# A sliding-window copy with twelve staged batches, half-row direct copies and the remainders on SP's queue

## The chip, the core and the metric

The kernel runs on one core of a Trainium2 chip. It does no arithmetic: it only moves data with DMAs, which 16 DMA engines of the core carry out. Three sequencers issue the DMAs: SP (SyncE) and ACT (ScalarE) each feed a hardware queue, POOL (GpSimd) feeds a queue whose descriptors are written by software. All three queues run on the same 16 engines. The metric is the device time of one execution in microseconds; less is better.

## The reference

The input x has 32 batches of 4096 rows of 256 float32 values (134 MB). Windows of 64 rows start every 32 rows, 127 of them per batch, and each is copied out.

```python
n_windows = (length - window_size) // stride + 1      # 127
for i in range(n_windows):
    start = i * stride                                # stride 32
    result[:, i] = x[:, start:start + window_size]    # window 64
```

The output is 32 x 127 x 64 x 256 float32, 266.3 MB. A batch is 128 blocks of 32 rows (32 KB each). Window w is block w followed by block w + 1, so each block but the first and last is written twice: as the first half of one window and as the second half of the one before it.

## The kernel before

**Two ways to copy a batch.** A *direct* batch is copied from HBM to HBM. A row of such a DMA is one window, 64 KB in one piece on both sides (Copier.windows with half=None), and the engines move it as two packets of 32 KB (DIRECT). Windows can also be copied by halves: one DMA for the first halves of a group of windows and one for the second halves (half 0 and 1), with rows of 32 KB, one packet each. A direct batch reads each block twice. A *staged* batch is loaded to SBUF once, in a tile of 128 partitions, one block to each (Copier.load, rows of 32 KB in packets of 16 KB, IN), and stored twice, once as all first halves and once as all second halves (Copier.store, packets of 16 KB, OUT).

**Which batches.** Eleven batches are staged: 1, 4, 7, ..., 28 and 30. The other 21 are direct. Staged batches go on ACT's queue, direct ones on SP's.

**The spill.** A staged store writes all 128 blocks as first halves and all 128 as second halves, though there are only 127 windows. The last first half falls on window 0 of the next batch, and the first second half on window 126 of the batch before. Those windows hold wrong bytes until the direct neighbour writes them, so the neighbour must write them after the staged store has landed. A direct batch therefore has 7 chunks of 16 windows that touch no spill (112 windows), and a *remainder* of 15 windows at the end or at the beginning (rest_parts), which waits for the staged neighbour's stores (waits, Staging.wait_stored). The last staged batch doesn't spill: it is stored in pieces of 112, 15, 15 and 112 rows. In the kernel before this is batch 30.

**Staging on ACT's queue.** There are 6 tiles. Staging.run goes through the staged batches in groups of 6: all loads of a group, then all its stores. A load into a used tile waits until that tile's stores have landed; a store waits for its load.

**Direct copies on SP's queue.** SP issues the 7 chunks of each of the 21 direct batches in order and doesn't wait. A running count, share, decides whether a chunk goes as one DMA of whole windows (1024 KB) or two DMAs of halves (512 KB each): by halves in 9 of 12 while the count of turns falls in the stretch of loads, in 3 of 12 otherwise. A *turn* here is one packet that an engine takes from the queue; the small packet that marks a DMA as complete is one too. So a chunk as a whole takes 2 + 1 turns on each engine, by halves 2 x (1 + 1).

**Remainders on POOL's queue.** When the chunk third from the end has landed (semaphore near), POOL issues the 21 remainders, 15 windows (960 KB) each, in the order of the staged batches that they wait for. SP ends with waits for everything: the direct copies (done), POOL's remainders (soft) and the last staged batch (last).

Of the kernel before, what the change touches and what calls it, by code (L numbers as in the profile page):

```python
# [6 lines left out]


DIRECT, IN, OUT = 32768, 16384, 16384
PIECES = (32768,)  # L10


class Copier:


    def __init__(self, nc, tc, x, out, B, L, D, W, S, n_win):
        assert W == 2 * S and L % S == 0
        self.nc, self.tc, self.x, self.out = nc, tc, x, out
        self.B = B
        self.blk = S * D  # L20
        self.nb = L // S
        self.nw = n_win
        self.total = 0
        self.done = tc.alloc_semaphore("done")
        self.last = tc.alloc_semaphore("last")
        self.last_total = 0

    def xap(self, block, dims):
        return bass.AP(self.x.tensor, self.x.offset + block * self.blk, dims)
# [4 lines left out]
    def count(self, dma):  # L34
        dma.then_inc(self.done, 16)
        self.total += 16

    def count_last(self, dma):
        dma.then_inc(self.last, 16)
        self.last_total += 16  # L40

    def windows(self, q, b, w0, n, half=None, piece=DIRECT, count=None):

# [21 lines left out]
    def store(self, q, t, b, half, p0=0, n=None):  # L65

        blk = self.blk
        n = self.nb if n is None else n  # L70
        w = b * self.nw + p0 - half
        return q.dma_start(
            out=self.oap(w * 2 * blk + half * blk, [[2 * blk, n], [1, blk]]),
            in_=t[p0 : p0 + n, :],
            max_dma_last_dim=OUT,
        )


class Staging:
# [14 lines left out]
    def store(self, q, g):  # L94
        n, i = divmod(g, len(self.tiles))
        q.wait_ge(self.loaded[i], 16 * (n + 1))
        if g == len(self.batches) - 1:

            for half, p0, rows in ((0, 0, 112), (0, 112, 15), (1, 1, 15), (1, 16, 112)):
                self.c.count_last(self.c.store(q, self.tiles[i], self.batches[g], half, p0, rows))  # L100
            return
        for half in (0, 1):
            self.c.store(q, self.tiles[i], self.batches[g], half).then_inc(self.stored[i], 16)
# [15 lines left out]
@with_exitstack  # L119
def kernel(  # L120
    ctx: ExitStack,
    tc: tile.TileContext,
    x: bass.AP,
    window_size: bass.AP,
    stride: bass.AP,
    out: bass.AP,
):
    nc = tc.nc
    W, S = int(window_size), int(stride)
    B, L, D = x.shape  # L130
    n_win = (L - W) // S + 1
    assert out.shape == (B, n_win, W, D)
    c = Copier(nc, tc, x, out, B, L, D, W, S, n_win)
    staged = [*range(1, B - 3, 3), B - 2]
    direct = [b for b in range(B) if b not in staged]
    pool = ctx.enter_context(tc.tile_pool(name="xb", bufs=1))
    st = Staging(c, pool, x.dtype, staged, 6)
    ring_d, ring_s = nc.sync, nc.scalar
    spilled = staged[:-1]

    waits = {b: [g for g, n in enumerate(spilled) if abs(n - b) == 1] for b in direct}
    per, loads, stores = 6, 6 * 17, 34

    def first(b):
        return 0 if b - 1 not in spilled else 8 if len(waits[b]) == 2 else 15

    def rest_parts(b):
        if len(waits[b]) == 2:
            return [(0, 8), (120, 7)]
        return [(0 if b - 1 in spilled else 112, 15)]  # L150

    soft = tc.alloc_semaphore("soft")
    soft_total = 0

    near = tc.alloc_semaphore("near")

    def mark(dma):
        dma.then_inc(near, 16)

    def count_soft(dma):  # L160
        nonlocal soft_total
        dma.then_inc(soft, 16)
        soft_total += 16

    with tc.tile_critical():  # L165
        st.run(ring_s)

        turns = share = 0
        rests = []
        todo = 7 * len(direct)  # L170
        for b in direct:
            for j in range(7):
                at = turns % (loads + per * stores)
                share += 9 if at < loads else 3
                if share >= 12:
                    share -= 12
                    turns += 4
                    c.windows(ring_d, b, first(b) + 16 * j, 16, 0)
                    c.windows(ring_d, b, first(b) + 16 * j, 16, 1, count=mark if todo == 3 else None)
                else:  # L180
                    turns += 3
                    c.windows(ring_d, b, first(b) + 16 * j, 16, count=mark if todo == 3 else None)
                todo -= 1
            rests.append(b)

        ring_r = nc.gpsimd
        ring_r.wait_ge(near, 16)
        for i, b in enumerate(sorted(rests, key=lambda b: max(waits[b], default=0))):
            for g in waits[b]:
                st.wait_stored(ring_r, g)  # L190
            for w, n in rest_parts(b):
                c.windows(ring_r, b, w, n, None, PIECES[i % 1], count_soft)
        ring_d.wait_ge(c.done, c.total)
        ring_d.wait_ge(soft, soft_total)
        ring_d.wait_ge(c.last, c.last_total)


# [33 lines left out]
```

## Time and profile before

| | |
|---|---|
| time, three runs | 745.32, 745.44, 745.96 us (median 745.44) |
| the profiled execution | 745.32 us |
| its span | 743.5 us |
| bytes moved by the DMA engines | 313.16 MB in 18,092 packets |
| HBM read / written | 220.92 / 266.99 MB |
| SP's DMAs | 83 of 1024 KB, 128 of 512 KB |
| ACT's DMAs | 11 loads and 20 stores of 4096 KB, 2 stores of 3584 KB, 2 of 480 KB |
| POOL's DMAs | 21 of 960 KB |

The page cuts the span in 40 slices and gives for each the busy share of the 16 DMA engines in tenths, and the GB/s that they moved. A byte that goes from HBM to HBM counts once in those bytes, but is one byte read and one written for HBM. The queue table gives for each queue its packets, its bytes and the time that its packets took, as a share of 16 engines times the span. q1 is SP's queue, q10 is ACT's and q0 is POOL's. Packets under 512 bytes are the completion marks. The same tables can be asked of any stretch of the span. The busy times of POOL on this page are those of issuing instructions; no engine computes.

### The profile page before, as it was taken

Reading aid. Unit: us, or ns where it says so; the run is one execution under the profiler, and the core shown is the slowest. Engines: PE = TensorE matmul, PEld = TensorE weight load, DVE = VectorE, ACT = ScalarE, POOL = GpSimd, SP = SyncE. Lnnn points to the kernel's source line nnn. Section 1 sums busy time; section 2 is a strip of 40 time slices with the busy share of each in tenths; the row PEclk is TensorE's granted clock in tenths of the full one; section 3 lists DMA queues with packets and bytes.
Section 4 is the critical chain, followed back from the end, with each engine's and each line's share of the span. In section 5 each row is a group of like instructions: output and inputs, shape, how many; then the busy total and the mean of one; then the engine's idle time right before and its main releaser. Section 6 shows DMA issues by size and latency. Waiting matters only on the chain.

```text
span 743.5 us, 321 instructions
## 1 busy us (share of the span) xinstructions
POOL 12.4 (2%) x25
## 2 busy tenths in 40 slices
POOL 0000000000000000000000000000000000050000
DMA  8999999999999999999999999999999999999995
GB/s 368 431 430 427 426 436 436 423 440 420 431 432 425 427 438 420 435 427 421 439 423 408 431 434 432 434 424 433 427 437 429 430 425 437 421 435 432 414 420 191
DMA packets 18092, 313.16 MB, mean 421 GB/s; under 512 B 4312, under 2 KB 4312, under 8 KB 4312
## 3 DMA queue, kind: packets, MB, share of 16 engines
q1 hardware_dynamic: 8080, 154.15, 48.5%
q10 hardware_dynamic: 9002, 138.35, 43.8%
q0 software_dynamic: 1008, 20.65, 6.8%
q14 instruction: 2, 0.02, 0.0%
HBM read 220.92 MB, written 266.99 MB: 656 GB/s over the span
## 4 chain that ended last, share of the span: by engine, by line
another core or an unknown queue 91%; POOL 2%; issue 0%; POOLq 0%; SPq 0%
POOL out_dram L48 2%; POOLq L226 0%; SPq L165 0%; POOLq L107 0%
## 5 line engine op out<-in xcount | busy, mean ns | idle before, releaser
L48 POOL DMA_DIRECT2D out_dram<-in_x_dram x21 | 12.2, 584 | 674.3 <-DMA out_dram<-in_x_dram 651.4
L212 POOL MEMSET const-float32-0.0<- 128x1 f32 x1 | 0.1, 93 | 0.2 <-issue 0.2
L212 POOL MEMSET const-bfloat16-1.0<- 128x1 bf16 x1 | 0.1, 97 | 0.0
L212 POOL MEMSET const-uint8-127<- 128x1 uint8 x1 | 0.1, 93 | 0.0
L212 POOL MEMSET const-float32-1.0<- 128x1 f32 x1 | 0.1, 92 | 0.0
## 6 DMA issues: line engine op xcount, KB each, us to landing
out_dram<-in_x_dram SPq DMA_DIRECT2D x83, 1024.0 KB, 97.1
out_dram<-xb ACTq DMA_DIRECT2D x20, 4096.0 KB, 137.8
out_dram<-in_x_dram SPq DMA_DIRECT2D x128, 512.0 KB, 90.5
xb<-in_x_dram ACTq DMA_DIRECT2D x11, 4096.0 KB, 122.1
out_dram<-in_x_dram POOLq DMA_DIRECT2D x21, 960.0 KB, 46.5
out_dram<-xb ACTq DMA_DIRECT2D x2, 3584.0 KB, 127.3
out_dram<-xb ACTq DMA_DIRECT2D x2, 480.0 KB, 112.8
```

Source lines behind the costliest of these rows:

```text
L48: q.dma_start(out=self.oap((b * self.nw + w0) * 2 * blk + off, [[2 * blk, n], [1, size]]), in_=bass.AP(self.x.tensor, self.x.offset + (b * ...
L212: nc = _bacc.Bacc("TRN2", target_bir_lowering=False, num_devices=1)
```

## The change

- Batch 0 becomes the twelfth staged batch, the last in the list. So it is batch 0 that is stored in pieces of 112, 15, 15 and 112 rows, and batch 30 now spills. The direct batches are 20. Batch 29 stands between two spilling batches: its remainder is cut in two pieces, of 8 windows at the beginning and 7 at the end.
- The share of chunks that go by halves is 12 of 12 while the count of turns falls in the loads, and 11 of 12 otherwise: 132 chunks by halves (264 DMAs), 8 whole.
- The remainders no longer go on POOL's queue. SP issues them among its direct chunks: after each batch, the function rest looks which remainders may go by now, that is, whether the count of turns is 34 past the turn at which the staged neighbour's stores should have ended (stored_turn). For each of them SP waits for those stores and then issues the remainder. What is left at the end is issued then, with the same waits.
- The semaphores near, soft and last go; all direct copies and the last staged batch count on done.

On ACT's queue nothing else changes: one more load and one more pair of stores, in two full groups of 6. The diff:

```diff
-PIECES = (32768,)
...
-    def count_last(self, dma):
-        dma.then_inc(self.last, 16)
-        self.last_total += 16
...
             for half, p0, rows in ((0, 0, 112), (0, 112, 15), (1, 1, 15), (1, 16, 112)):
-                self.c.count_last(self.c.store(q, self.tiles[i], self.batches[g], half, p0, rows))
+                self.c.count(self.c.store(q, self.tiles[i], self.batches[g], half, p0, rows))
...
-    staged = [*range(1, B - 3, 3), B - 2]
+    staged = [*range(1, B - 3, 3), B - 2, 0]
...
+    def stored_turn(b):
+        return max(
+            [(g // per) * (loads + per * stores) + loads + (g % per + 1) * stores for g in waits[b]],
+            default=0,
+        )
 
     with tc.tile_critical():
         st.run(ring_s)
 
         turns = share = 0
         rests = []
-        todo = 7 * len(direct)
+
+        def rest(slack):
+            nonlocal turns
+            for b in list(rests):
+                if turns >= stored_turn(b) + slack:
+                    rests.remove(b)
+                    for g in waits[b]:
+                        st.wait_stored(ring_d, g)
+                    for w, n in rest_parts(b):
+                        c.windows(ring_d, b, w, n)
+                        turns += 3
+
         for b in direct:
             for j in range(7):
                 at = turns % (loads + per * stores)
-                share += 9 if at < loads else 3
+                share += 12 if at < loads else 11
                 if share >= 12:
                     share -= 12
                     turns += 4
                     c.windows(ring_d, b, first(b) + 16 * j, 16, 0)
-                    c.windows(ring_d, b, first(b) + 16 * j, 16, 1, count=mark if todo == 3 else None)
+                    c.windows(ring_d, b, first(b) + 16 * j, 16, 1)
                 else:
                     turns += 3
-                    c.windows(ring_d, b, first(b) + 16 * j, 16, count=mark if todo == 3 else None)
-                todo -= 1
+                    c.windows(ring_d, b, first(b) + 16 * j, 16)
             rests.append(b)
-
-        ring_r = nc.gpsimd
-        ring_r.wait_ge(near, 16)
-        for i, b in enumerate(sorted(rests, key=lambda b: max(waits[b], default=0))):
-            for g in waits[b]:
-                st.wait_stored(ring_r, g)
-            for w, n in rest_parts(b):
-                c.windows(ring_r, b, w, n, None, PIECES[i % 1], count_soft)
+            rest(34)
+        rest(-10000)
         ring_d.wait_ge(c.done, c.total)
-        ring_d.wait_ge(soft, soft_total)
-        ring_d.wait_ge(c.last, c.last_total)
```

More of the change, by code (lines that the diff above doesn't have):

```diff
@@ L24, in __init__ @@
         self.done = tc.alloc_semaphore("done")
-        self.last = tc.alloc_semaphore("last")
-        self.last_total = 0
     def xap(self, block, dims):
@@ L150, in rest_parts @@
         return [(0 if b - 1 in spilled else 112, 15)]
[L152 to L163, printed above, removed]
+    def stored_turn(b):
[3 more added lines that the diff above has]
+        )
     with tc.tile_critical():
```

## The prediction

> **What bounds the kernel now.** Nothing computes here, so I read the page's slices and queue table first, then stretches of the timeline, then the queue table of a quiet, a busier and a late stretch.
>
> ```profile
> DMA  8999999999999999999999999999999999999995
> DMA packets 18092, 313.16 MB, mean 421 GB/s; under 512 B 4312, under 2 KB 4312, under 8 KB 4312
> q1 hardware_dynamic: 8080, 154.15, 48.5%
> q10 hardware_dynamic: 9002, 138.35, 43.8%
> q0 software_dynamic: 1008, 20.65, 6.8%
> HBM read 220.92 MB, written 266.99 MB: 656 GB/s over the span
> ```
>
> All DMA engines work from start to end. q1 is SP's queue of direct copies, q10 ACT's queue of staged loads and stores, q0 POOL's remainders. Now stretches: start:end, width, POOL busy, an unused clock, DMA share, GB/s.
>
> ```profile
> 0.00:20.00 20.00, 0.20 (x4) 1.00 0.93 382
> 20.00:160.00 140.00, 0.00 (x0) 1.00 1.00 429
> 160.00:410.00 250.00, 0.00 (x0) 1.00 1.01 428
> 410.00:550.00 140.00, 0.00 (x0) 1.00 1.01 431
> 660.00:720.00 60.00, 4.06 (x8) 1.00 1.00 425
> 720.00:736.00 16.00, 0.00 (x0) 1.00 0.93 343
> 736.00:743.50 7.50, 0.00 (x0) 1.00 0.03 13
> ```
>
> The engines move 425 to 431 GB/s whatever the mix, and less only at the end. The price of a packet comes from the queue table of 440 to 490 us:
>
> ```profile
> DMA packets 1306, 21.64 MB, mean 433 GB/s; under 512 B 336, under 2 KB 336, under 8 KB 336
> q1 hardware_dynamic: 654, 11.50, 53.6%
> q10 hardware_dynamic: 652, 10.14, 47.3%
> ```
>
> 16 engines times 50 us is 800 engine-us. q1 took 428.8 of them for 11.50 MB, which is 351 packets of 32 KB, and 303 small ones, the completion marks (9 ns each in the packet records): 1.214 us per 32 KB. q10 took 378.4 for 619 packets of 16 KB and 33 marks: 0.611 us. Per byte the two differ by 0.7%, so an engine has a fixed speed and **bytes moved through the engines are the bound, engine by engine**. The queues also get equal numbers of packets (654 and 652): an engine takes one from each in turn, marks included. I call this a turn.
>
> The last stretch, 722 to 732 us, shows the other limit:
>
> ```profile
> q0 software_dynamic: 155, 3.21, 90.5%
> q10 hardware_dynamic: 35, 0.38, 11.0%
> ```
>
> With hardly anything but direct copies, 98 packets of 32 KB take 144.8 engine-us, 1.48 us each. A direct copy reads and writes HBM for each byte moved, a staged one only one of the two.
>
> **The sum for the kernel before.** Data packets: (154.15 + 20.65) MB / 32 KB = 5334, and 138.35 MB / 16 KB = 8444; marks 4312. The mean engine has 333.4 x 1.214 + 527.8 x 0.611 + 269.5 x 0.009 = 404.7 + 322.5 + 2.4 = 729.6 us. The stretches show idle time of 1.4 us at the start (0.07 x 20), 1.1 in 720 to 736 and 7.3 after; 743.5 - 9.8 = 733.7 us busy. So 4.1 us went to packets slower than the quiet ones, some 2 of them in the stretch at 343 GB/s. By the packet records the last packet ends at 740.1 us on one engine alone, when most had ended near 735; 3.4 us of closing steps follow. The profiled execution took 745.32 us (1.8 above its span), the lowest of three and 0.12 below their median, so the sum needs no shift.
>
> **The change, part by part.**
>
> *A twelfth staged batch (batch 0).* It adds a load of 128 x 32 KB, 256 packets of 16 KB: 16 x 0.611 = 9.8 us on each engine. Its stores replace the same bytes of direct copies, at 2 x 0.611 for 1.214. ACT's queue now has 12 loads of 16, 11 pairs of stores of 32, and a last batch cut as before (28 packets per engine, plus 4 on those that take the 15-row pieces): 576 on a full engine. The HBM read falls from 220.92 MB to 12 x 4.19 + 20 x 8.32 = 216.8. I credit nothing for that: in 410 to 550 the packets already ran at their floor.
>
> *Direct chunks.* The 20 direct batches have 7 chunks of 16 rows: 140 rows of two 32 KB packets, 280 on each engine, however they are cut. Cutting nearly all into half-window DMAs only adds marks: SP issues 264 halves, 8 whole chunks and 21 remainder pieces, 293 in place of 211 (+21 on POOL). An engine has 331 marks in place of 269.5: +0.6 us. Is a half-row DMA itself dearer? 440 to 490 issued both kinds (8 of 512 KB, 10 of 1024 KB), and the price is the floor. Issuing costs nothing on the path: SP's DMAs land a median of 90 to 97 us after issue, so tens of them stand queued. That cover would be gone only if SP stopped for about as long.
>
> *The same, by a page.* The Trainium skill, "DMA: Bandwidth & Descriptors", section Rules for kernel authors, asks for at least 1 MiB per DMA, and its anatomy section fits about 2.0 us of fixed cost to one; 61 more DMAs would be an estimated 122 us by that if nothing overlapped, against the 0.6 us of the rows above.
>
> *The remainders go from POOL's ring to SP's queue.* This is the term that decides. While POOL's ring ran them (660 to 720) the DMA share was 1.00; were one engine of 16 left out, it would be near 0.94. So the software ring spread 15-row pieces over all 16. A hardware queue doesn't split so: ACT's 9002 packets are 8444 data and 558 marks; its 33 even DMAs make 528, so the two 15-row stores made 30, 15 engines each. Are they always the same 15? No row tells. If they rotate, an engine has 5080 / 16 = 317.5 packets of 32 KB and the floor is 385.4 + 351.8 + 3.0 = 740.2. If they are fixed, and the 8- and 7-row pieces also begin at the first engine, seven engines carry 280 + 19 x 2 + 2 + 2 = 322, and one carries 280 and idles some 53 us. Then the floor of the seven is 322 x 1.214 + 576 x 0.611 + 331 x 0.009 = 390.9 + 351.9 + 3.0 = 745.8. I take the fixed set: all the even DMAs give one share to every engine from the same start, and nothing in the counts shows a cursor that is carried on.
>
> The page named above says, in its section on how many engines a DMA uses, that a hardware queue uses the lowest-numbered k engines, k dividing the outer size; no run so far shows which.
>
> *Waits.* SP now waits for staged stores ahead of each remainder, with all later direct copies queued behind it. By turns, the first wait stands at SP's turn 194 for a store that ends at turn 136, the next ones keep 53 to 59, and the last, for the eleventh staged batch (turn 578), stands at 606. With equal turns, 28 turns at least (some 35 us of engine time with ACT's share) remain queued when SP goes on: nothing runs dry, cost 0; if it did, ACT's stores would still feed the engines. The wait on POOL (22.9 us) goes with its ring. Batch 0's load waits for the sixth staged store, with five loads queued in front: 0.
>
> *Slow packets.* SP and ACT have 615 and 614 turns on a full engine, so they end together and the direct-only end goes. Half of the bytes are direct all along: q1 moved 54% of them in 410 to 550 (32.54 of 60.32 MB, at 431 GB/s), and 57% in 160 to 410 (60.49 of 106.91, at 428). Against the floor's 313.16 / 729.6 = 429 GB/s, that is -3 to +2 us over the whole; nearest are 410 to 550 and 20 to 160 (431 and 429), so I take -1.
>
> **Sum.** 1.4 (start) + 745.8 - 1 + 1 (estimate, the slowest of seven equal engines) = 747.2 us for the last packet, against 740.1; + 3.4 = a span of 750.6; + 1.8 = **752.4 us**, 0.9% slower. With -3 to +2, and 0 to 4 for the slowest engine, 749.5 to 757.
>
> **Rivals.**
> - *The 15 engines rotate.* 1.4 + 740.2 - 1 + 1 + 3.4 + 1.8 = 746.8 us, at the edge of no change. For it: POOL's ring evens out. Against: it is another ring, and the marks show another split (378 / 21 = 18 per DMA). 0.12.
> - *HBM is the real bound (faster).* If time went with HBM bytes, 483.9 in place of 487.9 MB, the span would be 737.4 and the time 739.2. For it: 1.48 us per packet in the direct-only end. Against: the floor price at 53 to 54% direct. It decides only if packets still get faster below that share. 0.04.
> - *The queues end apart (slower).* If turns are not equal, or SP stands at the last wait with nothing queued, direct copies remain alone at the end, at 359 GB/s where 431 went: 50 us of such work take 60, so 762 us. Against: the 2890 and 2883 packets that the two queues had from 160 to 400 us would not stay so equal. It decides once over 25 us are left alone. 0.08.
>
> **How the numbers follow.** My case has 0.76. The range, 746.5 to 757.5, takes in the rotating case and its own bounds. About 0.2% (1.5 us) is what a measurement can tell from no change. Slower: 0.76, 0.08 and some 0.04 of the rotating case, 0.88; same: most of what remains of that, 0.07; faster: 0.05.
>
> **What the profile after would show.** 317.4 MB, 14,292 data packets, no q0; 1.21 and 0.61 us per packet; equal packets in q1 and q10 until the end; a DMA share near 0.94 in the last 50 us or spread over the span, and marks of 15 per remainder. Wrong if the share stays at 1.00 to the end (rotation), or if a stretch of q1 alone follows q10.

## The result and the profile after

The changed kernel takes **754.42 us** (753.03 to 755.05) where the kernel before takes 745.38 us: a ratio of 1.0117, 95% interval 1.0100 to 1.0135, so 9.0 us slower. The prediction said 752.4 us, in a range of 746.5 to 757.5. The profiled execution took 754.30 us, with a span of 752.5. In two of the three groups of experiments below the kernel before itself took 754 to 755 us, 1.3% more than here, for a reason that no run shows; so each ratio is to runs of the kernel before in its own group. In the third group the changed kernel was only 0.3% slower.

The page after, slices and queues, then the stretches, in the columns used in the prediction:

```profile
DMA  9999999999999999999999999999999999999995
...
DMA packets 19552, 317.43 MB, mean 422 GB/s; under 512 B 5258, under 2 KB 5258, under 8 KB 5258
...
q1 hardware_dynamic: 9732, 166.48, 51.7%
q10 hardware_dynamic: 9818, 150.93, 47.3%
...
HBM read 216.79 MB, written 267.06 MB: 643 GB/s over the span
```

```profile
20.00:160.00 140.00, 0.00 (x0) 1.00 1.00 430
160.00:410.00 250.00, 0.00 (x0) 1.00 1.01 430
410.00:550.00 140.00, 0.00 (x0) 1.00 1.00 430
...
690.00:700.00 10.00, 0.00 (x0) 1.00 0.98 408
700.00:710.00 10.00, 0.00 (x0) 1.00 1.02 419
...
715.00:740.00 25.00, 0.00 (x0) 1.00 0.95 393
...
736.00:752.50 16.50, 0.00 (x0) 1.00 0.45 193
```

What to see: 4.27 MB more go through the engines, though HBM is read 4.13 MB less. From 20 to 550 us all 16 engines are busy at 430 GB/s, steadier than before (428 to 431). The rows count a packet where it starts, so a stretch of 10 us can read 0.98 or 1.02 with all engines busy; they are busy up to 710 us. The end is longer: from 715 to 740 us the share is 0.95, near that of 15 engines of 16 (0.94), and the last 16 us are less than half used, because the engines stop one after another.

The marks fit the split that the prediction counted on. q1 has 166.48 MB / 32 KB = 5080 data packets, so 4652 marks; 272 DMAs of 16 marks, 19 of 15, one of 8 and one of 7 are 4352 + 285 + 15 = 4652.

To see *which* engines the pieces went to, I chained the packet records, each packet to the one that starts where it ends. At a tie the chain can swap two engines, so a chain's counts are rough; the times at which the 16 chains end are firmer (us):

```
kernel after:  713  740.3 741.4 741.8 742.2 742.9 742.9 743.6 743.8   744.8 745.5 745.5 746.0 746.5 747.2 750.9
```

One engine stops some 30 us early, eight between 740 and 744, seven between 744.8 and 751. The fixed set demands this grouping: one engine with 280 packets of 32 KB, eight with 318 or 320, seven with 322. By its packets at their floor the first engine should stop 53 us before the seven; it stops some 33 us before six of them. From 679 us on it has nothing left of SP's queue, and its last 28 packets of 16 KB, those of the last staged batch, took 34 us in place of 17. (Two expectations below put these slow packets at 671 to 726 us; the records have them from 679 to 713.)

### The profile page after: what moved, and what is told of

Its sections match the earlier page's. It is cut to its first block, busy times and chain, and to the rows that moved or that the text cites. A ratio compares the mean times of both kernels' runs of the same rounds, so it can differ in the third digit from the quotient of the medians.

```text
span 752.5 us, 382 instructions
## 1 busy us (share of the span) xinstructions
POOL 0.2 (0%) x4
## 3 DMA queue, kind: packets, MB, share of 16 engines
q1 hardware_dynamic: 9732, 166.48, 51.7%
```

## The experiments

### Each part alone, and the twelve batches with POOL's ring

**The remainders back on POOL**, everything else as changed:

```diff
...
-            rest(34)
-        rest(-10000)
...
+        ring_r = nc.gpsimd
+        ring_r.wait_ge(near, 16)
+        for b in sorted(rests, key=lambda b: max(waits[b], default=0)):
+            for g in waits[b]:
+                st.wait_stored(ring_r, g)
+            for w, n in rest_parts(b):
+                c.windows(ring_r, b, w, n, None, DIRECT, count_soft)
...
```

> The changed kernel with one part undone: the remainders go at the end on POOL's ring, as in the kernel before; twelve staged batches and half-row copies stay. Theory (engine by engine): the twelfth batch alone costs what the whole change costs. POOL's ring spreads evenly, so the floor is the mean engine's 740.2 us; the kernel before took 15.7 us more than its own mean floor (745.3 - 729.6), so 755.9 us here, at most 2 us from the changed kernel. Rival (the remainders on 15 fixed engines are a cost that the change adds to the batch): 5.6 us less than the changed kernel, 748.8 us.

Measured: 750.7 us, ratio 1.0077 (1.0055 to 1.0098), against 745.1 for before. Neither number: it lies 5.2 under the theory, 1.9 over the rival. Stretches of its end:

```profile
690.00:700.00 10.00, 0.00 (x0) 1.00 1.01 428
700.00:720.00 20.00, 1.71 (x3) 1.00 1.00 403
720.00:736.00 16.00, 0.00 (x0) 1.00 1.01 431
```

The share stays at 1.00: all 16 engines work to the end, and their chains end within 737.8 and 745.0 us with none early. This control shows that the remainders on SP's queue, not the new batch, make one engine stop early. Two things follow.

- *Twelfth batch and half rows together cost 5.6 us* (750.7 - 745.1), not the 10.4 of their floor (9.8 + 0.6). The rest came back where the kernel before had lost time: 720 to 736 us now runs at 431 GB/s in place of 343 (16 x (1 - 343/431) = 3.3 us), and 160 to 410 at 430 in place of 428 (1.2 us). My theory had carried the whole loss of the kernel before over to this one, and so missed by 5.
- *The remainders on SP cost some 3.7 us* (754.42 - 750.7, or 1.0117 against 1.0077; the two were measured in two groups, and their profiled executions differ by 4.1). The last packet comes 6.0 us later (750.9 against 745.0; the floors differ by 5.6). But the span ends 1.6 us after the last packet where it ends 3.4 us after it with POOL's ring: 1.8 us are given back.

**The remainders on SP alone**, on the kernel before (eleven batches, old share of halves):

```diff
-    staged = [*range(1, B - 3, 3), B - 2, 0]
+    staged = [*range(1, B - 3, 3), B - 2]
...
-                share += 12 if at < loads else 11
+                share += 9 if at < loads else 3
```

> The kernel before with one part done: the remainders go on SP's queue; eleven staged batches and the old share of half rows stay. Theory (15 fixed engines): an engine has up to 294 + 42 = 336 packets of 32 KB and 528 of 16 KB, a floor of 732.9 us; the changed kernel took 8.5 us more than its floor of 745.8 (754.3), so 741.4 us: faster than before by 4. Rival (the 15 engines rotate): the changed kernel took 14.2 us more than its mean floor of 740.2, so 729.6 + 14.2 = 743.8 us. Rival (waits on SP and slow packets eat it): 745 us or more.

Measured: 746.46 us, ratio 1.0015 (0.9996 to 1.0034): no change that can be told. The engine split is the fixed one again, one chain ending at 697 us and fifteen from 737 to 743, with the DMA share falling the same way:

```profile
160.00:410.00 250.00, 0.00 (x0) 1.00 1.01 424
...
690.00:700.00 10.00, 0.00 (x0) 1.00 0.97 408
700.00:720.00 20.00, 0.00 (x0) 1.00 0.96 396
720.00:736.00 16.00, 0.00 (x0) 1.00 0.94 397
```

One engine is left out here too, as the fixed set has it; the allowance over the floor was too small. With 56% of the bytes direct (174.80 of 313.16 MB) and remainders among them, 160 to 410 runs at 424 GB/s where the changed kernel, from which the allowance was taken, has 430: 3.5 us. From 550 to 660 it is 428 against 432, another 1.0. The rival of slow packets held, and the faster time of 741 didn't come.

**Half rows alone**, on the kernel before:

```diff
-                share += 9 if at < loads else 3
+                share += 12 if at < loads else 11
```

> The kernel before with one part done: nearly all direct chunks go by half rows; eleven staged batches, remainders on POOL at the end. The bytes of every engine stay as they are. Theory (equal turns, and direct copies alone are slower): SP's turns rise from 505 to about 588 against ACT's 563, so that SP and POOL have some 88 turns, 44 packets of 32 KB per engine, left when ACT ends; at 1.48 in place of 1.214 us that costs 11.7 us, so 757 us. Rival (half rows only add marks): 746 us.

Measured: 758.03 us, ratio 1.0168 (1.0124 to 1.0213). The theory held, 757 forecast. Not one byte was added; only the turns shifted, and ACT's queue ended at 675 us. The queue table of 700 to 740 us shows POOL's direct copies alone:

```profile
DMA packets 642, 13.21 MB, mean 330 GB/s; under 512 B 239, under 2 KB 239, under 8 KB 239
...
q0 software_dynamic: 642, 13.21, 99.5%
```

403 packets of 32 KB took 636.8 engine-us less 2.2 for marks: 1.57 us each in place of 1.214. This run shows that the turns decide which queue ends first, and that direct copies alone are slow. That HBM is what slows them fits, since each byte is read there and written there, but is not shown apart. The engines count as busy all the while; the price of a packet is what tells.

**The twelfth batch alone**, on the kernel before (the staged list of the change, nothing else):

> The kernel before with one part done: the twelfth staged batch; the old share of half rows and the remainders on POOL at the end stay. Theory (bytes per engine, 9.8 us for the batch, of which the removed direct-only end gives back some 4, as in the run with the remainders on POOL, 750.7): SP and POOL have about 541 turns against ACT's 614, so ACT's queue is alone at the end; if staged packets alone keep their 0.611 us the time is 750.7 us again, within 1.5. Rival (half rows are needed, because a queue alone is slow, as one engine's 16 KB packets of 0.7 to 1.6 us from 671 to 726 us in the changed kernel suggest): 755 us or more.

Measured: 775.83 us, ratio 1.0264 (1.0223 to 1.0305), in a group where before takes 754.4. The rival's time held, but not its reason. Without the half rows SP and POOL have some 546 turns (7728 and 1008 packets over 16 engines) against ACT's 614, and ACT's queue is alone in much of the end; its queue table from 707 to 714 us, and from 730 to 750:

```profile
DMA packets 195, 3.00 MB, mean 428 GB/s; under 512 B 12, under 2 KB 12, under 8 KB 12
...
q10 hardware_dynamic: 194, 3.00, 99.9%
```

```profile
DMA packets 387, 5.65 MB, mean 283 GB/s; under 512 B 42, under 2 KB 42, under 8 KB 42
...
q10 hardware_dynamic: 387, 5.65, 100.8%
```

First 183 packets of 16 KB in 111.9 engine-us, 0.61 us each; then 345 in 322.6, 0.93 each. So being alone doesn't make them slow. The slow ones belong to the last staged batch, whose 508 packets begin near 729 us (more below); after 700 us they add 8.9 us to the mean engine, beside the 9.8 of the batch itself. With half rows twelve batches cost 0.8% over the kernel before (1.0077), without them 2.6%, some 14 us more, though in another group. So the half rows, which cost 13 us with eleven batches, pay with twelve: the parts of the change can't be priced one by one and added.

### Sixteen equal shares

```diff
+    def spread(self, q, b, w0, n):
+        blk, cut = self.blk, 2 * self.blk // 16
+        self.count(
+            q.dma_start(
+                out=self.oap((b * self.nw + w0) * 2 * blk, [[cut, 16], [2 * blk, n], [1, cut]]),
+                in_=self.xap(b * self.nb + w0, [[cut, 16], [blk, n], [1, cut]]),
+            )
+        )
...
-                        c.windows(ring_d, b, w, n)
+                        c.spread(ring_d, b, w, n)
```

> The changed kernel with the remainders cut so that all 16 engines get the same: each DMA has an outer dimension of 16 pieces of 4 KB of a row, and 15 rows inside. By the line through the two packet times (0.611 us for 16 KB, 1.213 for 32 KB) a 4 KB packet takes 0.16 us. Theory (15 fixed engines in the changed kernel): the floor falls from the seven engines' 745.8 to 742.7 us on all (339.9 + 300 x 0.16 + 351.9 + 3.0), so 3.1 us less than the changed kernel, 751.2 us. Rival (they rotate already): 2.5 us more than the changed kernel, 756.9 us.

Measured: 777.15 us, ratio 1.0427 (1.0379 to 1.0474). It doesn't decide the question: a 4 KB packet does take 0.159 us at the median (0.16 forecast), but a remainder is now 16 turns in place of 3, ACT gets a 16 KB packet for each, ends early, and from 660 to 736 us direct copies run alone at 323 to 332 GB/s. I had counted bytes and forgotten turns. The fixed set is settled by the ends of the chains and by the control with POOL's ring.

### Why staged packets alone were slow

**Staged copies alone** (direct = []):

> The changed kernel without the direct copies (20 batches and all remainders are left out): ACT's queue alone. Theory A (ACT's queue alone is slow, 1.2 to 1.5 us per 16 KB packet as on one engine from 671 to 726 us in the changed kernel): 576 packets x 1.35 = 778 us. Theory B (a packet keeps 0.611 us alone, and those slow ones have another cause): 352 us, up to 380 with the waits for tiles.

Measured: 368.56 us, between the two, near the second. From 300 to 330 us, and in the last stretch, 335 to 355:

```profile
DMA packets 842, 13.01 MB, mean 434 GB/s; under 512 B 48, under 2 KB 48, under 8 KB 48
...
q10 hardware_dynamic: 842, 13.01, 101.2%
```

```profile
DMA packets 436, 6.36 MB, mean 318 GB/s; under 512 B 48, under 2 KB 48, under 8 KB 48
...
q10 hardware_dynamic: 436, 6.36, 100.1%
```

794 packets at 0.611 us, then 388 at 0.82. A queue alone isn't slow; the last batch's stores, of 112, 15, 15 and 112 rows, are.

**The same with the last batch in stores of 128 rows:**

```diff
-            for half, p0, rows in ((0, 0, 112), (0, 112, 15), (1, 1, 15), (1, 16, 112)):
+            for half, p0, rows in ((0, 0, 128), (1, 0, 128)):
...
-    staged = [*range(1, B - 3, 3), B - 2, 0]
+    staged = list(range(1, 24, 2))
```

> Staged copies alone again (direct copies and remainders left out), twelve other batches (1, 3, ..., 23), and the last one stored in two stores of 128 rows like all others, in place of 112, 15, 15 and 112 rows (so its spill is left wrong). The run before it took 368.6 us, and its packets were slow only in its last 30 us, which are the last batch's stores, 6.2 us more per engine than at 0.611. Theory (those stores are slow because of their row counts): 362 us, and no slow stretch at the end. Rival (a queue that runs out is slow at its end): 368 us.

Measured: 358.74 us. The slow end is gone; 330 to 350 us:

```profile
DMA packets 558, 8.62 MB, mean 431 GB/s; under 512 B 32, under 2 KB 32, under 8 KB 32
...
q10 hardware_dynamic: 558, 8.62, 100.5%
```

526 packets at 0.611 us, and 3 us less than the theory. The two runs, one execution of each, differ by 9.8 us. Of these, 6.0 are slower packets (8.2 us over 0.611 on the mean engine in the run above, 2.2 here), and most of the rest is that the engines ended unevenly: the last at 365.2 us with the mean at 360.5, here 355.4 and 354.4. So stores of 112 and 15 rows are slow when ACT's queue is alone. They need not be where direct packets go between: in the changed kernel the last 14 packets of 16 KB, the second store of 112 rows, took 0.611 us each on all engines but the one that stops early. The Trainium skill, "DMA: Bandwidth & Descriptors", section The descriptor swizzle, shows a transfer to 128 partitions in which each engine writes one SBUF port; that 112 or 15 rows break such a pairing would fit, but no run here shows ports.

**The changed kernel without the two 15-row stores:**

```diff
-            for half, p0, rows in ((0, 0, 112), (0, 112, 15), (1, 1, 15), (1, 16, 112)):
+            for half, p0, rows in ((0, 0, 112), (1, 16, 112)):
```

> The changed kernel without the two 15-row stores of the last staged batch (30 half windows of batch 0 stay unwritten). Four packets of 16 KB less on 15 engines are 2.4 us of floor. Theory (these stores and their slow packets make the last engine late): 2.4 + about 3 us less than the changed kernel, 749 us where that takes 754.4. Rival (the last engine is late for another reason): 752.0 us.

Measured: 755.21 us in a group where the changed kernel takes 757.88 (below): 2.7 us less, the four packets and hardly more. The rival held. Its last engine ends at 752.3 us, 3.3 after the next. So the 15-row stores don't make the last engine late; whether the 112-row ones do, and why one engine alone is late, stays open.

### The changed kernel in a slower group

> The changed kernel once more, beside the run without the 15-row stores on the same chip. If the chip is like the first one: 754.4 us, 1.2% above the kernel before. On a chip where the kernel before takes 754 us, as in the second group of runs: theory (an engine's packets, fewer HBM bytes, so less lost where HBM is slower): less than 1.2% above before; rival (time follows bytes per engine alone): 1.2%.

Measured: 757.88 us, ratio 1.0031 (1.0012 to 1.0051), beside 755.3 for the kernel before. The first theory's time held; its reason, fewer HBM bytes, is argued, since no run changes these bytes alone. From one group to the other the kernel before lost 10 us, the changed one 3.5. Queue tables of 160 to 410 us, of the changed kernel in the first group, and again here:

```profile
DMA packets 6580, 107.47 MB, mean 430 GB/s; under 512 B 1756, under 2 KB 1756, under 8 KB 1756
...
q1 hardware_dynamic: 3288, 56.86, 53.3%
```

```profile
DMA packets 6520, 106.63 MB, mean 427 GB/s; under 512 B 1732, under 2 KB 1732, under 8 KB 1732
...
q1 hardware_dynamic: 3259, 56.37, 53.1%
```

and of the next kernel, nearly the kernel before, in the same group:

```profile
DMA packets 5819, 105.12 MB, mean 420 GB/s; under 512 B 1241, under 2 KB 1241, under 8 KB 1241
...
q1 hardware_dynamic: 2912, 60.23, 57.8%
```

With 53% of the bytes direct the engines keep 427 GB/s here; with 57% they fall to 420, where the kernel before, at 57% too, had 428 in the first group.

### Three attempts at a faster kernel

**Fewer half rows in the kernel before**, so that no direct copies are left at the end (share += 7 and 2 in place of 9 and 3):

> The kernel before with 48 of its 147 chunks by half rows in place of 64: SP and POOL have 552 turns in place of 568 against ACT's 563. Theory (queues that end together): the direct-only end goes (16 us at 343 in place of 431 GB/s, 3 us), 2 us faster than before, 743.4 where that takes 745.4. Rival (ACT's last stores are then alone at the end, and slow): 2 us slower or more.

Measured: 756.45 us, ratio 1.0020 (1.0006 to 1.0033). The direct-only end did go (412 GB/s in 720 to 736 us), and the time didn't fall: it lies between theory and rival, 1.2 us over the kernel before. ACT's queue now ends last, at 750.6 us, 6 us after POOL's, as the rival had it. More whole chunks also raise the direct share all along, to 57.3% of the bytes from 160 to 410 (56.6 before); which of the two ate the gain isn't settled, since the kernel before has no profile in this group.

**POOL's remainders as their neighbours land**, on the kernel before, its wait for near left out:

```diff
-        ring_r.wait_ge(near, 16)
```

> The kernel before with the remainders still on POOL's ring, but issued as soon as the staged neighbours have landed, in place of all at the end. Theory (even engines, no direct copies left alone at the end): floor of the mean engine 729.6, 4.8 us of start and slow packets as in the run with twelve staged batches and POOL's remainders (745.0 - 740.2), some 3 more because direct copies are 56% of the bytes, 5.2 us of closing: 742.6 us. Rival (a third queue all along takes turns from ACT, so that staged copies end late and alone, or the direct share rises over 58%): 745 us or more.

Measured: 772.93 us, ratio 1.0251 (1.0213 to 1.0288). The rival held. The queue table of 180 to 200 us, when a remainder runs beside the other queues:

```profile
DMA packets 405, 7.72 MB, mean 386 GB/s; under 512 B 102, under 2 KB 102, under 8 KB 102
...
q0 software_dynamic: 131, 2.75, 36.4%
q1 hardware_dynamic: 139, 2.75, 34.5%
q10 hardware_dynamic: 135, 2.21, 29.1%
```

Three queues share the turns equally, two of them direct: 71% of the bytes, 386 GB/s, and 1.31 us per 32 KB packet on q1 (110.4 engine-us less marks, over 84). ACT, pushed back, ends last with its slow stores, at 775 us (POOL at 765). The wait for near in the kernel before, which looks idle, keeps two direct queues apart.

**Ten staged batches**, all chunks whole, POOL as in the last one:

> Ten staged batches, all direct chunks as whole windows (so that SP's and POOL's 528 turns stand against ACT's 512), remainders on POOL as their neighbours land. Theory (bytes per engine are the bound): the floor is 719.5 us, + 4.8, + 5 for slow packets at a direct share of 59%, + 5.2 = 734.5 us. Rival (HBM takes back what the engines save: packets slow down once direct copies pass 58% of the bytes): 745 us.

Measured: 776.86 us, ratio 1.0289 (1.0270 to 1.0307). It moves 8.5 MB less through the engines than the changed kernel and is slower, at 403 GB/s from 160 to 410 us. The theory failed; the rival had the direction but not the size (745 where before takes 745.4). The direct share and the third queue were changed together here, so their parts aren't separated. No version here beats the kernel before.

## Why the prediction was right, point by point

- **The bound.** Bytes per engine at fixed packet prices: held. In 440 to 490 us of the profile after, 346 packets of 32 KB took 424 engine-us less 2.9 for marks, 1.217 us (1.214 forecast), and 626 of 16 KB 0.612 us (0.611).
- **The fixed 15 engines**, which I took without a row to decide it: shown, by the three groups of ends, by the one early engine with the remainders on SP alone, and by the control with POOL's ring, where no engine stops early. The share near 0.94 that the prediction named as its sign came from 715 to 740 us (0.95). The rotating rival (746.8 us) falls. The page's sentence on the lowest-numbered engines is borne out as far as "always the same"; which ones the records don't name.
- **The floor of the seven**, 745.8 us, put the last packet at 747.2. Six of the seven ended from 744.8 to 747.2. The term that failed is "+ 1, the slowest of seven equal engines": the slowest came 3.7 us later than the sum, at 750.9, so that this term is 4.7, where the range allowed 0 to 4; why is open. The 53 us that one engine idles were some 33, since its last 28 packets were slow; that cost nothing.
- **The closing**, + 3.4, carried over from the kernel before, was mis-sized the other way: 1.6 us without POOL's ring. The two errors, +3.7 and -1.8, partly cancel, which is luck, and leave 752.4 against 754.3 profiled.
- **Waits on SP at cost 0:** held. SP waited 126.2 us in ten waits, of 17.5 at the longest, and 41.2 at the last remainders, and its queue did not run dry: from 690 to 740 us q1 and q10 had 603 and 623 packets.
- **Slow packets, -1:** on the 15 engines that set the time, packets took 3.7 us more than at their floor, against some 4.4 us by which an engine's packets overlap: -0.7. Right in the group of the result. In the third group the changed kernel is only 0.3% behind, so a credit was due there; that it is for fewer HBM bytes is not shown.
- **The estimate by the page**, 122 us for 61 more DMAs, did not come: from 20 to 550 us the changed kernel, with nearly all direct chunks in DMAs of 512 KB, ran at 430 GB/s. The page fits its 2.0 us to DMAs of the software queue; these are queued on SP's.
- **The queues end apart:** not at the end of this kernel, but it is the rival that the half rows alone (758.0) and the sixteen shares (777.2) ran into. Direct copies alone moved some 330 GB/s there, less than the 359 that the prediction took.

So the 9.0 us are 5.6 for the batch with its half rows (10.4 of floor, 4.8 won back from the end and from slow packets) and 3.7 for the remainders on SP (6.0 on the engines, 1.8 won back in the closing, by the profiled executions); what is left over lies between groups and executions.

## What to carry to other kernels

When DMA engines are the bound, add up each engine's packets, not the kernel's bytes: the pieces of 15 rows on SP's hardware queue left the same engine out each time, and stores of 112 and 15 rows were slower than those of 128 where nothing went between them. Queues that share the engines take equal packets, so packet size and count set the mix. With direct copies at 53% of the bytes the engines moved 430 and 427 GB/s in two groups, at 57% 428 and 420: keep them near half, and let the queues end together. A part that is a loss by itself (half rows, + 13 us) can be what makes the next part bearable. And measure a gain or loss of 1% in more than one group of runs: this one was 1.2% in one and 0.3% in another.

## What had not been expected of the hardware

- The span ends 3.4 us after the last packet with POOL's ring in use (before, and with twelve batches and POOL), 1.6 to 1.7 us without it (after, the remainders on SP alone, without the 15-row stores).
- Stores of 112 and 15 rows from SBUF, with no other queue at work: 0.82 us per 16 KB packet where 128-row stores take 0.611, and 9.8 us in all on one batch. With direct packets between them they can run at 0.611.
- The same kernel took 745 us in one group of runs and 754 to 755 in two others, and the changed kernel, with 2% less HBM traffic per byte moved (483.9 / 317.4 against 487.9 / 313.2) and an even mix, lost a third of that (3.5 in place of 10 us); the cause is open.
- One engine ends 3 to 4 us after all others in the changed kernel and in that without the 15-row stores, two engines (754.2 and 755.2 us, the next at 750.7) in the changed kernel's second group; the cause is open.
